# A hybrid decoder layer on one core: the low parts of the up projection's weights, subtracted by VectorE or added by a transfer

## The chip, the cores and the metric

The kernel runs on one core of a Trainium2 chip. The metric is the time of one execution on the device in microseconds. A core has a matrix engine (TensorE, PE in the profile), a vector engine (VectorE, DVE), a scalar engine (ScalarE, ACT), a general engine (GpSimd, POOL) and a synchronization engine (SyncE, SP). Each works through its own list of instructions in order, and semaphores make one wait for another. SP and GpSimd also start transfers (DMAs) between the outer memory and the memory on the chip; 16 DMA engines carry them out.

## The reference, cut to what matters

One step of a decoder layer for 512 prompt rows and 8 sample rows, 520 in all. After three mixing branches and a first layer norm comes a gated feed-forward block:

```
h = layer_norm(ALPHA * x + merged @ w_o)                     # 520 x 1024
u = causal_dwconv(h @ w_ffn_in, width 3)                     # 520 x 5632
f = (silu(u[..., :D_FF]) * u[..., D_FF:]) @ w_ffn_out        # D_FF = 2816
out = layer_norm(ALPHA * h + f)
```

All of it is in float32. The change concerns the weights of `h @ w_ffn_in`, the gated product's up projection.

## The kernel before

Everything stands transposed: features on the 128 partitions, the 520 rows along the free dimension, in two halves of 260 columns.

TensorE multiplies in a rounded float32 format (fp32r). To keep the precision, every operand is split into a rounded high part and a low part that holds the rest, and every product is three matmuls: high by high, high weight by low data, low weight by high data (`mm3`, where line 357 issues the matmul). `split` makes the parts: ScalarE rounds the source into `hi` by a copy (`act`, line 161), VectorE subtracts it from the source into `lo` (`tt`, line 164).

The up projection has 5632 output features, that is 44 units of 128. A unit's weights are a tile of 128 x 1024: eight blocks of 128 x 128. Per unit, `wunit` loads the tile by a transfer on SP's queue into `raw` (line 241; two buffers), and `wsplit` splits it into `whi` and `wlo` (two buffers each). Then come 48 matmuls: 2 halves by 8 blocks by 3. A unit can be split when TensorE is through with the unit two before, whose buffers it takes. When `raw` has been read for the last time, SP loads the unit after next, and behind it starts a copy of a piece of a cache (line 219) that has nothing to do with the unit.

The result of each half is evicted by ScalarE twice (`ffn_evac`): a plain copy `fu` and a scaled one `fy`. `ffn_taps` adds the two other taps of the width-3 convolution on VectorE (line 167) and has GpSimd copy ten columns aside (line 1465). Units come in pairs, gate and up; `silu` on ScalarE and a product on VectorE follow, and the result is split into `f` for the down projection.

The first six units (`NH`, the list `early`) are special. They are loaded and split while the first layer norm still runs, two into `whi` and `wlo`, four into spare tiles named `wz`, each as two halves of 128 x 512. Their matmuls are done for the first 260 columns and then for the second, so that TensorE has work while the second half is normalized. The layer norm (`proj_ln`) writes its rows into `r`, rounds them on ScalarE into `h_hi` and subtracts on VectorE into `h_lo`.

The order on each engine is set when the program is built: a scheduler with a model of times places the instructions by priority (`hp` gives weight splits and evictions a high one, the dense matmuls have a low one).

Of the kernel before, what the change touches and what calls it, by code (L numbers as in the profile page):

```python
# [12 lines left out]
ALU = mybir.AluOpType  # L13
# [103 lines left out]
def build(tc, nc, I, O):  # L117
    V, S, T, G = nc.vector, nc.scalar, nc.tensor, nc.gpsimd
# [11 lines left out]
    def hp(more=0):  # L130
        return tc.high_priority(HP + more)
# [13 lines left out]
    def z2(name, shape=(128, NT), dt=F32):  # L145
        return pool.tile(list(shape), dt, tag="z", bufs=NZ, name=name)
# [13 lines left out]
    def act(out, in_, func=AF.Copy, **kw):  # L160
        return S.activation(out, in_, func, **kw)  # L161

    def tt(out, a, b, op):
        return V.tensor_tensor(out, a, b, op=op)  # L164
# [50 lines left out]
    def cache_step(n=1):  # L215
        for _ in range(n):
            pc = next(pieces, None)
            if pc is not None:
                nc.sync.dma_start(*pc)

    nload, last_split, quiet = [0], [None], [False]

    def split(hi, lo, src):
        act(hi, src)
        return tt(lo, src, hi.bitcast(F32), ALU.subtract)
# [12 lines left out]
    def wload(src, n):  # L238
        raw = wp.tile([128, 8, 128], F32, tag="raw", bufs=2, name="raw")
        with tc.issue_after(x_load.ins):  # L240
            ins = nc.sync.dma_start(raw[:, :n].rearrange("p k m -> p (k m)"), src)
        nload[0] += 1
        if nload[0] > 1 and late:
            with tc.issue_after(ins.ins):
                late.popleft()()
        elif nload[0] > 6:
            with tc.issue_after(ins.ins):
                cache_step(0 if quiet[0] else 3 if nload[0] % 4 == 0 else 1)
        return raw

    def wsplit(raw, n, where=None):

        if where is None:
            where = [[wp.tile([128, 8, 128], F32R, tag=t, name=t) for t in ("whi", "wlo")]]
        ks, k0 = [], 0
        for hi, lo in where:
            m = min(hi.shape[1], n - k0)
            if m > 0:
                last_split[0] = split(hi[:, :m], lo[:, :m], raw[:, k0:k0 + m])
                ks += [(hi[:, k], lo[:, k]) for k in range(m)]  # L260
            k0 += m
        return ks

    def wunit(src, n, where=None):
        with hp():
            return wsplit(wload(src, n), n, where)

    def wz(*allocs):

        return [[alloc("wz", (128, 4, 128), F32R) for _ in range(2)] for alloc in allocs]  # L270
# [18 lines left out]
    def P(name, i=0, n=1):  # L289
        o = PPO[name] + i  # L290
        return pp[:, o:o + n]
# [68 lines left out]
    def dps(n=2):  # L360
        return [pd.tile([128, 512], F32, tag="d", name="ps")[:, :HB] for h in range(n)]


    def densemm(ps, w, X, first=True, last=True, halves=(0, 1)):
        with tc.high_priority(-LOW):
            mm3(ps, w, X, first, last, halves)

    def dense(w, X):
        ps = dps()
        densemm(ps, w, X)  # L370
        return ps
# [3 lines left out]
    def zchunk():  # L375
        i = zi[0]
        zi[0] += 1
        w = w0 if i == 0 else wunit(I['wz'][i], 8)
        return dense(w, XS)
# [744 lines left out]
    def stream_dense():  # L1124
# [61 lines left out]
        def branch(i, js, na):  # L1186
            br = B_ORDER[i]
            wn, X, n, ev = outs[br]
            ahead = []
            for j in js[:na]:  # L1190
                ahead.append(gate(br, j))
                yield 6.5
            yield ('w', ev)
            for j in js:
                gt = ahead[j] if j < len(ahead) else gate(br, j)
                w = wunit(I[wn][j], n)
                pb = dense(w, X)
                if i == 0:
                    mg.append(gt)
                if i == 2:  # L1200
                    XM.append((t2(f"m{j}h", dt=F32R), t2(f"m{j}l", dt=F32R)))
                with hp():
                    for h in range(2):
                        stt(gt[:, HS[h]], gt[:, HS[h]], 1.0, pb[h], ALU.add, ALU.mult)

                for sl in HS if i == 2 and j == 7 else (slice(0, NT),):
                    if i:
                        tt(mg[j][:, sl], mg[j][:, sl], gt[:, sl], ALU.add)
                    if i == 2:
                        hi, lo = [x[:, sl] for x in XM[j]]  # L1210
                        act(hi, mg[j][:, sl], scale=0.5)
                        last_m[0] = stt(lo, mg[j][:, sl], 0.5, hi.bitcast(F32), ALU.mult, ALU.subtract)
                yield 6.5 + 0.8 * n
# [214 lines left out]
    XH = [(h_hi[:, j, :], h_lo[:, j, :]) for j in range(8)]  # L1428
# [4 lines left out]
    def wo_unit(j):  # L1433
        q = j - nF1
        where = wz(z2, z2) if 2 <= q < 6 else wz(t2, t2) if q == 6 else wz(a2, a2) if q == 7 else None

        quiet[0] = True
        with ExitStack() as es:
            if j:
                es.enter_context(tc.issue_after(last_m[0].ins))  # L1440
            r = [(wunit(I['wo'][j], 8, where), 0)]
        quiet[0] = False
        if j in range(1, 6):
            nc.sync.dma_start(rr[j + 1], I['xT'][:, j + 1, :])
        return r
# [18 lines left out]
    def ffn_taps(c, u, y):  # L1464
        G.tensor_copy(nu[:, c, :], u[:, 510:520])  # L1465
        tt(y[:, 512:520], y[:, 512:520], sfs[:, c, :], ALU.add)
        stt(y[:, 1:512], u[:, 0:511], P('fdw', c * 3 + 1), y[:, 1:512])
        stt(y[:, 2:512], u[:, 0:510], P('fdw', c * 3 + 0), y[:, 2:512])

    def ffn_evac(c, u, y, ps, halves):  # L1470
        with hp():
            for h, p_ in zip(halves, ps):
                act(u[:, HS[h]], p_)
            for h, p_ in zip(halves, ps):
                act(y[:, HS[h]], p_, AF.Identity, scale=P('fdw', c * 3 + 2), bias=P('fdb', c))

    early = []
    for i in range(NH):
        early.append((wunit(I['wfi'][i], 8, (wz(t2, a2) if i > 3 else wz(z2, z2)) if i >= 2 else None), z2("fu"), z2("fy")))
    for h in range(2):  # L1480
        for i in range(NH):
            w, u, y = early[i]
# [7 lines left out]
    def ffn_chunk(c, i):  # L1490
        if i < NH:
            _, u, y = early[i]
        else:
            u, y = z2("fu"), z2("fy")
            ffn_evac(c, u, y, dense(wunit(I['wfi'][i], 8), XH), (0, 1))
        ffn_taps(c, u, y)
        return y

    for i in range(22):
        yg = ffn_chunk(i, 2 * i)  # L1500
        act(yg, yg, AF.Silu)
        yu = ffn_chunk(22 + i, 2 * i + 1)
        tt(yg, yg, yu, ALU.mult)
        hi, lo = [t(f"f{i}", dt=F32R) for t in FT[i]]
        split(hi, lo, yg)
        XF.append((hi, lo))
# [123 lines left out]
```

## Time and profile before

| | |
|---|---|
| time, median of 3 runs | 1019.94 us (1019.75 to 1020.02) |
| profiled execution | 1019.17 us, its span 1017.4 us |
| TensorE busy | 991.1 us (97%) |
| VectorE busy | 712.7 us (70%) |
| ScalarE busy | 498.1 us (49%) |
| GpSimd busy | 217.6 us (21%) |
| mean granted clock of TensorE | 0.992 |
| moved by DMA | 153.07 MB, mean 150 GB/s |

The span is the time from the first to the last instruction of the profiled execution. Busy times are sums over the span, so an engine with a low share can still be the one that is waited for in some stretch. Matmuls overlap: one is shown with 0.28 us while the next starts 0.12 us later. The granted clock is given as a share of the full 2.4 GHz.

### The profile page before, as it was taken

The numbers are of one execution on the slowest core, as the hardware profiler recorded it, in microseconds if no ns is written. First come the engines' busy times: TensorE is split into PE (matmuls) and PEld (weight loads), VectorE is DVE, ScalarE is ACT, GpSimd is POOL, SyncE is SP. The second block draws the span as 40 slices with busy tenths as digits, with TensorE's granted clock in tenths as the row PEclk, the third lists the DMA queues.
The fourth block names the chain that finished last, engine by engine and source line by source line (L and its number), as shares of the span: only waits on it lengthen the run. The fifth ranks groups of instructions, "written<-read, shape, count | busy, mean of one in ns | idle before, by whom it ended". The sixth has DMA issues, their size and how long they took to land.

```text
span 1017.4 us, 22069 instructions
## 1 busy us (share of the span) xinstructions
PE 991.1 (97%) x8979; PEld 965.6 (95%) x8979; DVE 712.7 (70%) x1335; ACT 498.1 (49%) x1029; POOL 217.6 (21%) x313
## 2 busy tenths in 40 slices
PE   7999999999999999999999998999999999999994
PEld 7999999999999899989999997999999999999994
DVE  5999899996587589873657888655565655423286
ACT  6345843574453444355543466555555555312154
POOL 0131355363414533321011000111111111000000
PEclk9999999999999999999999998999999999999998
DMA  7543356666536767564346441134334343332322
GB/s 245 198 158 119 135 170 216 208 193 230 190 102 180 242 213 247 158 194 140 120 138 241 151 166 63 53 115 139 116 123 143 115 140 114 113 95 81 96 74 84
DMA packets 48501, 153.07 MB, mean 150 GB/s; under 512 B 9808, under 2 KB 13456, under 8 KB 45328
## 3 DMA queue, kind: packets, MB, share of 16 engines
q1 hardware_dynamic: 35520, 113.15, 33.9%
q0 software_dynamic: 12880, 38.52, 11.7%
q8 instruction: 70, 1.15, 0.5%
q14 instruction: 31, 0.25, 0.1%
HBM read 132.02 MB, written 46.81 MB: 176 GB/s over the span
## 4 chain that ended last, share of the span: by engine, by line
PE 82%; DVE 7%; DMA 4%; issue 3%; ACT 3%; POOL 1%; SPq 0%; ACTq 0%; POOLq 0%; DVEq 0%
PE ps L357 72%; DVE r L167 1%; DVE wlo L164 1%; PE lor L423 1%; PE at L640 1%; ACT whi L161 1%; DVE vx L164 1%; DMA raw<-in_wrw_dram 1%; DMA swk<-in_swkv_dram 0%; PE q L794 0%; PE pt L496 0%; PE st L821 0%; DMA sct<-nd 0%; DMA raw<-in_wz_dram 0%; PE btp L655 0%
## 5 line engine op out<-in xcount | busy, mean ns | idle before, releaser
L357 PE MATMUL ps<-x_hi,whi 128*128 128x260 f32 x1024 | 292.2, 285 | 5.6 <-ACT whi L161 5.5
L357 PE MATMUL ps<-x_lo,whi 128*128 128x260 f32 x1024 | 293.0, 286 | 0.3 <-DVE x_lo L164 0.2
L357 PE MATMUL ps<-x_hi,wlo 128*128 128x260 f32 x1024 | 292.5, 286 | 0.4 <-DVE wlo L164 0.4
L164 DVE TENSOR_TENSOR wlo<-raw,whi 128x1024 fp32r<-128x1024 f32 (+2 forms) x152 | 168.4, 1108 | 173.2 <-ACT whi L161 172.4
L161 ACT ACTIVATE whi<-raw 128x1024 fp32r<-128x1024 f32 (+2 forms) x152 | 146.9, 967 | 221.6 <-PE ps L357 195.7
L357 PEld LDWEIGHTS ps<-x_hi,whi 128*128 128x128 f32 x1024 | 193.6, 189 | 6.9 <-ACT whi L161 5.5
L357 PEld LDWEIGHTS ps<-x_hi,wlo 128*128 128x128 f32 x1024 | 194.0, 189 | 2.4 <-DVE wlo L164 1.0
L357 PEld LDWEIGHTS ps<-x_lo,whi 128*128 128x128 f32 x1024 | 193.4, 189 | 1.8 <-DVE x_lo L164 1.1
L357 PE MATMUL ps<-h_lo,whi 128*128 128x260 f32 x640 | 182.1, 284 | 4.0 <-DVE h_lo L164 4.0
L357 PE MATMUL ps<-h_hi,whi 128*128 128x260 f32 x640 | 181.2, 283 | 0.0
L357 PE MATMUL ps<-h_hi,wlo 128*128 128x260 f32 x640 | 180.6, 282 | 0.0
L357 PEld LDWEIGHTS ps<-h_lo,whi 128*128 128x128 f32 x640 | 120.7, 189 | 4.6 <-DVE h_lo L164 4.4
L357 PEld LDWEIGHTS ps<-h_hi,wlo 128*128 128x128 f32 x640 | 121.1, 189 | 0.1
L357 PEld LDWEIGHTS ps<-h_hi,whi 128*128 128x128 f32 x640 | 120.6, 188 | 0.0
L357 PE MATMUL ps<-f,whi 128*128 128x260 f32 x592 | 107.2, 282 | 0.0
L1465 POOL COPY nu<-fu 128x10 f32<-128x10 f32 x44 | 40.3, 916 | 270.9 <-ACT fu L161 270.9
L357 PEld LDWEIGHTS ps<-f,whi 128*128 128x128 f32 x592 | 91.4, 188 | 0.1
L167 DVE SCALAR_TENSOR_TENSOR acc<-u,pp,acc 128x511 f32<-128x511 f32 (+29 forms) x120 | 84.3, 733 | 0.4
L357 PE MATMUL ps<-f,wlo 128*128 128x260 f32 x296 | 83.6, 283 | 0.0
L167 DVE SCALAR_TENSOR_TENSOR fy<-fu,pp,fy 128x511 f32<-128x511 f32 x88 | 65.8, 747 | 1.5
L357 PEld LDWEIGHTS ps<-f,wlo 128*128 128x128 f32 x296 | 55.7, 188 | 0.0
L161 ACT ACTIVATE fu<-ps 128x260 f32<-128x260 f32 x88 | 33.0, 377 | 43.4 <-PE ps L357 43.3
(549 smaller groups left out, 1841.3 us busy)
## 6 DMA issues: line engine op xcount, KB each, us to landing
raw<-in_wz_dram SPq DMA_DIRECT2D x63, 512.0 KB, 3.7
raw<-in_wfi_dram SPq DMA_DIRECT2D x44, 512.0 KB, 3.5
out_dram<-in_cc_dram SPq DMA_DIRECT2D x128, 128.0 KB, 3.5
rl<-d POOLq DMA_DIRECT2D x32, 256.0 KB, 4.9
raw<-in_wfo_dram SPq DMA_DIRECT2D x16, 512.0 KB, 3.6
out_dram<-in_cb_dram SPq DMA_DIRECT2D x56, 146.0 KB, 3.7
d<-at POOLq DMA_DIRECT2D x16, 256.0 KB, 3.6
raw<-in_wo_dram SPq DMA_DIRECT2D x8, 512.0 KB, 3.7
```

The source lines that it names most:

```text
L161: return S.activation(out, in_, func, **kw)
L164: return V.tensor_tensor(out, a, b, op=op)
L167: return V.scalar_tensor_tensor(out, a, s, b, op0=op0, op1=op1)
L357: last_mm[0] = T.matmul(ps[i], lhsT=a, rhs=x[:, HS[h]], start=first and k == 0 and q == 0, stop=last and k == len(w) - 1 and q == 2)
L423: T.matmul(ps, lhsT=lor[l][w][:, p, :], rhs=X[x][:, HS[h]], start=i == 0, stop=i == len(wx) - 1)
L640: T.matmul(pst[par][:, c * 128:(c + 1) * 128], lhsT=bk[o:o + 64, c].rearrange("p a b -> p (a b)"), rhs=kr[o:o + 64, c].rearrange("p a b -> ...
L1465: G.tensor_copy(nu[:, c, :], u[:, 510:520])
```

## The change

For the 44 units of the up projection the low part is made in another way. Before, VectorE computed `lo = raw - hi`. Now ScalarE, after rounding `raw` into `hi`, makes a second pass and writes the negative of the same rounded value into `lo`; then GpSimd starts a transfer that reads the unit's weights from the outer memory once more and adds them onto `lo`, so that it holds `raw - hi` when the transfer has landed. The splits of all other weights and of the data are as before. The outer memory is read for 44 x 512 KB more.

```diff
-    def wsplit(raw, n, where=None):
+    def wsplit(raw, n, where=None, src=None):
...
             if m > 0:
-                last_split[0] = split(hi[:, :m], lo[:, :m], raw[:, k0:k0 + m])
+                w = raw[:, k0:k0 + m]
+                if src is None:
+                    last_split[0] = split(hi[:, :m], lo[:, :m], w)
+                else:
+                    act(hi[:, :m], w)
+                    act(lo[:, :m], w, scale=-1.0)
+                    G.dma_start(lo[:, :m].rearrange("p k m -> p (k m)"), src[:, k0 * 128:(k0 + m) * 128],
+                                accum_op=ALU.add)
...
-    def wunit(src, n, where=None):
+    def wunit(src, n, where=None, add=False):
         with hp():
-            return wsplit(wload(src, n), n, where)
+            return wsplit(wload(src, n), n, where, src if add else None)
...
     for i in range(NH):
-        early.append((wunit(I['wfi'][i], 8, (wz(t2, a2) if i > 3 else wz(z2, z2)) if i >= 2 else None), z2("fu"), z2("fy")))
+        early.append((wunit(I['wfi'][i], 8, (wz(t2, a2) if i > 3 else wz(z2, z2)) if i >= 2 else None,
+                            0 <= i <= 5), z2("fu"), z2("fy")))
...
-            ffn_evac(c, u, y, dense(wunit(I['wfi'][i], 8), XH), (0, 1))
+            ffn_evac(c, u, y, dense(wunit(I['wfi'][i], 8, add=6 <= i <= 43), XH), (0, 1))
```

First place: ScalarE in the middle of the up projection, two units. Before, it held this, with `whi` the rounding of a unit, `fu` and `fy` the evictions of one half, and `f` and the second `fy` parts of the gating:

```order
L161 ACTIVATE f_9528<-fy 128x520 [waits DVE_49]
L161 ACTIVATE whi<-raw 128x1024 [waits DMAHW2_49,PE_49]
L161 ACTIVATE fu<-ps 128x260 [waits PE_49]
L161 ACTIVATE fy<-ps,pp 128x260
L161 ACTIVATE fu<-ps 128x260 [waits PE_49,Pool_49]
L161 ACTIVATE fy<-ps,pp 128x260
L161 ACTIVATE fy<-fy 128x520 [waits DVE_49,Activation_49]
L161 ACTIVATE whi<-raw 128x1024 [waits DMAHW4_49,PE_49]
```

Now it holds this, at the same place of the stage:

```order
L161 ACTIVATE whi<-raw 128x1024 [waits DMAHW4_49,PE_49]
L161 ACTIVATE fu<-ps 128x260 [waits PE_49]
L161 ACTIVATE fy<-ps,pp 128x260
L161 ACTIVATE wlo<-raw 128x1024 [waits DMASW1_49,Activation_49]
L161 ACTIVATE fu<-ps 128x260 [waits PE_49,Pool_49]
L161 ACTIVATE fy<-ps,pp 128x260
L161 ACTIVATE fy<-fy 128x520 [waits DVE_49,Activation_49]
L161 ACTIVATE whi<-raw 128x1024 [waits DMAHW6_49,PE_49]
```

The pass into `wlo` stands behind one pair of evictions, three instructions after the rounding.

Second place: GpSimd in the same stage, where before there stood 44 copies into `nu` and nothing between them. Now transfers (`DMA wlo<-in_wfi_dram`) alternate with the copies:

```order
L1473 COPY nu<-fu 128x10 [waits Activation_49]
L266 DMA wlo<-in_wfi_dram 128x1024 [waits DMASW1_49,PE_49,Activation_49]
L1473 COPY nu<-fu 128x10 [waits Activation_49]
L266 DMA wlo<-in_wfi_dram 128x1024 [waits DMASW2_49,PE_49,Activation_49]
L1473 COPY nu<-fu 128x10 [waits Activation_49]
```

Each transfer waits for ScalarE's pass. On TensorE the order in this stage is the one of before, but the first matmul of a unit that reads `wlo` now waits for a transfer (DMASW) where it waited for VectorE.

Third place: VectorE in the first layer norm, from the variance of the first half (`lrs<-lv,lm`) on. Before:

```order
L167 SCALAR_TENSOR_TENSOR lrs<-lv_7893,lm_8211 128x260 [waits PE_49]
L167 SCALAR_TENSOR_TENSOR r_7809<-ld_7892,r_7809 128x260
L164 TENSOR_TENSOR lsq<-lsq 128x260 [waits Activation_49]
L167 SCALAR_TENSOR_TENSOR r_7809<-r_7809,ps 128x260 [waits PE_49]
L164 TENSOR_TENSOR wlo<-raw,whi 128x1024 [waits DMAHW4_49,Activation_49]
L164 TENSOR_TENSOR r_7809<-r_7809,cn 128x260 [waits DVE_49]
L1373 RECIPROCAL lrs<-lrs 128x260 [waits Activation_49]
L164 TENSOR_TENSOR wz<-raw,wz 128x512 [waits DMAHW6_49,Activation_49]
```

Now:

```order
L167 SCALAR_TENSOR_TENSOR lrs<-lv_7893,lm_8211 128x260 [waits PE_49,Activation_49]
L167 SCALAR_TENSOR_TENSOR r_7805<-ld_7892,r_7805 128x260
L167 SCALAR_TENSOR_TENSOR r_7807<-ld_7892,r_7807 128x260
L167 SCALAR_TENSOR_TENSOR r_7809<-ld_7892,r_7809 128x260
L164 TENSOR_TENSOR lsq<-lsq 128x260 [waits Activation_49]
L167 SCALAR_TENSOR_TENSOR r_7809<-r_7809,ps 128x260 [waits PE_49]
L1381 RECIPROCAL lrs<-lrs 128x260 [waits Activation_49]
L164 TENSOR_TENSOR r_7809<-r_7809,cn 128x260 [waits DVE_49]
```

The subtractions into `wlo` and `wz` are gone from between the norm's own steps, and the variance comes ahead of two steps that it followed.

## Rows read from the trace of the kernel before

**Rows 1.** The page's head and its first part, busy us of each engine.

```profile
span 1017.4 us, 22069 instructions
PE 991.1 (97%) x8979; PEld 965.6 (95%) x8979; DVE 712.7 (70%) x1335; ACT 498.1 (49%) x1029; POOL 217.6 (21%) x313
```

**Rows 2.** Windows: stretch, length, busy of each engine, PEclk, DMA share, GB/s.

```profile
600.00:606.00 6.00, 6.00 (x52) 6.00 (x51) 5.99 (x12) 4.10 (x10) 0.00 (x0) 1.00 0.68 224
606.00:612.00 6.00, 6.00 (x52) 6.00 (x51) 6.00 (x16) 4.36 (x12) 0.00 (x0) 1.00 0.42 147
...
655.00:862.00 207.00, 207.00 (x1729) 207.00 (x1729) 123.27 (x182) 117.38 (x216) 34.19 (x36) 1.00 0.37 123
```

**Rows 3.** ScalarE's timeline at one unit: start us, duration us, what [idle before].

```profile
701.30 1.06 ACT L161 ACTIVATE whi<-raw 128x1024 fp32r<-128x1024 f32 x1 [1.18 <-PE ps L357]
702.26 0.37 ACT L161 ACTIVATE fu<-ps 128x260 f32<-128x260 f32 x1
702.53 0.56 ACT L161 ACTIVATE fy<-ps,pp 128x260 f32<-128x260 f32 x1
...
707.05 1.06 ACT L161 ACTIVATE whi<-raw 128x1024 fp32r<-128x1024 f32 x1 [0.50 <-PE ps L357]
```

**Rows 4.** VectorE's timeline at the same unit.

```profile
702.39 1.23 DVE L164 TENSOR_TENSOR wlo<-raw,whi 128x1024 fp32r<-128x1024 f32 x1 [3.00 <-ACT whi L161]
```

**Rows 5.** TensorE's timeline, two matmuls in a row of an up projection unit.

```profile
623.40 0.28 PE L357 MATMUL ps<-h_hi,wlo 128*128 128x260 f32 x1
623.52 0.28 PE L357 MATMUL ps<-h_hi,whi 128*128 128x260 f32 x1
```

**Rows 6.** Tile wlo in 655 to 860: duration ns min/median/max, first and last start.

```profile
L357 PE MATMUL ps<-h_hi,wlo x569: 277/282/286, 655.4 to 859.7; 128*128 128x260 f32 x190
L164 DVE TENSOR_TENSOR wlo<-raw,whi x35: 1224/1226/1229, 662.1 to 857.7; 128x1024 fp32r<-128x1024 f32 x35
```

**Rows 7.** ScalarE's timeline: the rounding of unit 6.

```profile
640.89 1.06 ACT L161 ACTIVATE whi<-raw 128x1024 fp32r<-128x1024 f32 x1 [4.79 <-PE ps L357]
```

**Rows 8.** VectorE's timeline in the layer norm: one whole and one half subtraction.

```profile
598.18 1.22 DVE L164 TENSOR_TENSOR wlo<-raw,whi 128x1024 fp32r<-128x1024 f32 x1 [0.49 <-ACT whi L161]
...
602.92 0.69 DVE L164 TENSOR_TENSOR wz<-raw,wz 128x512 fp32r<-128x512 f32 x1
```

**Rows 9.** TensorE's waits: whom for, us in total, times, longest.

```profile
PE ps L357 <- DVE h_lo L164: 4.0, 2, 3.3
```

**Rows 10.** TensorE's timeline at these waits.

```profile
613.48 0.39 PE L357 MATMUL ps<-h_lo,whi 128*128 128x260 f32 x1 [0.72 <-DVE h_lo L164]
613.71 0.28 PE L357 MATMUL ps<-h_hi,wlo 128*128 128x260 f32 x1
613.82 0.36 PE L357 MATMUL ps<-h_hi,whi 128*128 128x260 f32 x1
617.45 0.59 PE L357 MATMUL ps<-h_lo,whi 128*128 128x260 f32 x1 [3.26 <-DVE h_lo L164]
```

**Rows 11.** Windows after these waits.

```profile
616.00:620.00 4.00, 2.16 (x6) 1.67 (x7) 4.00 (x12) 2.56 (x7) 0.00 (x0) 0.50 0.72 229
620.00:624.00 4.00, 4.00 (x20) 3.51 (x19) 2.19 (x6) 1.67 (x5) 0.00 (x0) 0.67 0.01 4
```

**Rows 12.** GpSimd's timeline at the unit of rows 3.

```profile
702.69 0.98 POOL L1465 COPY nu<-fu 128x10 f32<-128x10 f32 x1 [4.78 <-ACT fu L161]
```

**Rows 13.** DMA issues: queue, count, size of each, median us from issue to landing.

```profile
raw<-in_wfi_dram SPq DMA_DIRECT2D x44, 512.0 KB, 3.5
...
raw<-in_wfo_dram SPq DMA_DIRECT2D x16, 512.0 KB, 3.6
...
raw<-in_wcv_dram SPq DMA_DIRECT2D x8, 256.0 KB, 2.8
...
nd<-scr POOLq DMA_DIRECT2D x1, 512.0 KB, 4.1
...
sct<-nd POOLq DMA_DIRECT2D x1, 256.0 KB, 8.7
```

**Rows 14.** SP's timeline at the unit of rows 3.

```profile
703.64 0.33 SPq L241 DMA_DIRECT2D raw<-in_wfi_dram  x1
```

## The prediction, made before the changed kernel ran

> **What bounds the kernel now.** I read the page's first part, then the busy times by stretch, then the timelines of one unit of the stage that changes. TensorE is busy in 991.1 of 1017.4 us [rows 1], and in the stage of the up projection, 655 to 862 us, in all of 207.00 us, while VectorE has 123.27 and ScalarE 117.38 [rows 2]. So a microsecond taken off VectorE there is worth nothing by itself; a microsecond put in front of TensorE costs a microsecond. The other place that matters is the layer norm before it: at 600 to 612 us VectorE is busy in 5.99 and 6.00 of each 6 us [rows 2], and shortly after TensorE waits for it.
>
> One unit (a weight tile of 128x1024, 48 matmuls) takes 5.75 us: the rounding of unit i starts at 701.30 and that of unit i+1 at 707.05, each when TensorE is through with the buffer of the unit two before [rows 3]. Two buffers of each kind take turns, so unit i-1 runs on TensorE from about 701.3 to 707.05, and within this time unit i must be made ready. Before, VectorE subtracts at 702.39 for 1.23 us [rows 4]: ready at 703.62. Every unit's matmuls come as high, high, low, spaced 0.12 us [rows 5], so the low part is read first at 707.05 + 0.24 = 707.29. The slack is 3.7 us, and no unit of the stage waits for its weights.
>
> **The change part by part.**
>
> *Removed:* 44 subtractions on VectorE. 36 of them (units 8 to 43; 35 show in the window, 1.226 us each [rows 6]) lie in the stage where TensorE never waits for VectorE: worth 0. The other eight units come earlier. Unit 6 is rounded at 640.89 [rows 7] and its low part first read at 655.4 [rows 6], and unit 7 is much the same: 0. Units 0 to 5 are split inside the crowded layer norm: two of 1.22 us and eight halves of 0.69 us [rows 8], 8.0 us of VectorE where TensorE waits 4.0 us for the low part of the normalized rows [rows 9], the longer of these waits ending at 617.45 [rows 10]. The granted clock is 0.50 in 616 to 620 and 0.67 in 620 to 624 [rows 11]; 0.67 over 4 us means half clock until about 622.6, so 5.2 us after 617.45 ran at half speed, 1.2 instead of 2.4 GHz: 2.6 us lost. At best 4.0 + 2.6 = 6.6 us come back. Against that ScalarE gets as many extra passes there (two of 1.06, eight of about 0.6: 6.9 us), in front of its own rounding of those rows; at worst all 6.9 us delay TensorE. I take half of the best, 3 us of gain.
>
> *Added on ScalarE:* one more pass of 1.06 us a unit [rows 3]. In the stage that makes 117.4 + 36 x 1.06 = 156 of 207 us, so it does not bind by itself. But it stands in the path of the low part, and behind the two evictions of the unit two before, as the order shows.
>
> *Added on GpSimd's queue:* a transfer of 512 KB a unit that adds onto the low tile. It can only be issued when the second pass is done, and TensorE's third matmul now waits for its landing. Its own queue does not hold it up: the copy between two transfers is done at 702.69 + 0.98 = 703.67 [rows 12], before the pass it stands ahead of is over.
>
> The path: rounding 701.30, evictions 702.26 and 702.53, the second taking 0.56 to 703.09 [rows 3], second pass 1.06 to 704.15, 0.06 from ScalarE to GpSimd (702.63 to 702.69 [rows 3, 12]): issue at 704.21. With another 0.06 for the wait at the end, the landing may take 707.29 - 704.21 - 0.06 = 3.0 us and no more. Call D what it takes.
>
> If D is over 3.0, unit i starts D - 3.0 late. Unit i+1 is not late a second time: its buffer came free at the end of unit i-1, before this gap, so its low part arrives with the same delay and finds unit i still running. So the pattern is two units back to back, then a gap: **18 gaps of D - 3.0 us for 36 units.**
>
> *D.* The trace has no adding transfer. The nearest rows [rows 13]: a plain 512 KB load on SP's queue lands in 3.5 us; a plain 512 KB one on GpSimd's in 4.1 (there is one); the slowest listed on it 8.7. Moving time is seen by size: 256 KB in 2.8 and 512 KB in 3.6 us on the same queue, so 1.6 us for 512 KB. An addition must fetch the old bytes besides the new: 1.6 more. And the next raw load, 512 KB, is issued by the same event (raw is read for the last time by what makes the low part: 703.64, against the subtraction's end at 703.62 [rows 14, 4]), so the two share the engines: between 0 and 1.6, I take 0.8. D = 4.1 + 1.6 + 0.8 = 6.5 us. Lower end 4.1, upper end 8.7 + 1.6 = 10.3.
>
> The Trainium skill puts the movement lower: "DMA: Bandwidth & Descriptors", section "Anatomy of one DMA — SWDGE (gpsimd) path", fits 2.0 us plus bytes over 436 GB/s, 3.2 us for 512 KB as an estimate; the one row here says 4.1 and decides. "Collectives: The Full Stack", section "The bandwidth ceiling: the fold count and why AG ≠ RS ≠ AR", says that the sum itself is free but its two reads halve the rate; no run here shows that yet. By both, D would be 2.0 + 2 x 1.2 = 4.4 us, 18 x 1.4 = 25 us of gaps and 1041 us by estimate, which is inside rival A below.
>
> *The clock.* A pause of 3.26 us with a handful of matmuls and 0.72 us before it brought the clock down and cost 2.6 us [rows 10, 11]. Gaps of 3.5 us between full stretches are of that size, but shorter than the whole pause there. I take a third of the 18: 6 x 2.6 = 16 us; the ends are 0 and 18 x 2.6 = 47.
>
> **Sum:** 18 x (6.5 - 3.0) = 63, plus 16, minus 3: +76 us. The profiled execution took 1019.17 us (1.8 around its span), the median is 1019.94, so 1095 by the one and **1096 us** by the other.
>
> **Rivals.**
>
> *A. The transfer is light.* D between 3.5 and 5.2: the old bytes come out of on-chip memory beside the new ones, at no price, and the raw load is no hindrance. 18 x 0.5 to 18 x 2.2, no falls of the clock, 0 to 7 back: about 1019 to 1060. For it: the plain row of 4.1. Against: it must move more bytes than that row and beside another load.
>
> *B. The transfer is heavy.* D over 8 (an add that goes by smaller pieces, or many bytes waiting in turn): every gap over 5 us, and the clock falls in each. From 18 x 5.0 + 47 - 3 = +134 to 18 x 7.3 + 47 + 7 = +185: 1153 to 1204. For it: GpSimd's transfers of 256 KB have taken up to 8.7. Against: that one is the slowest of the list.
>
> *C. Faster.* D at 3.0 or below: the stage costs nothing, and what is left is the relief of VectorE in the layer norm, up to 6.6 us: 1013 to 1019. It decides from D = 3.0. For it: VectorE is full there and TensorE waits. Against: even the plain load on SP's queue takes 3.5.
>
> *D. ScalarE binds.* 4.3 us of work in a unit of 5.75: no, unless its queue order makes a rounding wait behind a slow eviction; it would add at most the second pass, 1.06 x 36 = 38 us, and only where the transfer is hidden. I count it into A's and the forecast's upper ends.
>
> **How the numbers follow.** The forecast, D from 5.2 to 8, has its own range of 18 x 2.2 - 3 = +37 to 18 x 5.0 + 47 - 3 = +134, 1057 to 1153, with 0.58. A 0.16, B 0.20, C and a tie 0.06 (C itself 0.04). To hold eight in ten I go down through most of A and half of B: 1036 to 1185. Within 0.2% (2 us, about what a measurement of this kernel can tell from no change) I give 0.02, faster 0.04, slower 0.94.
>
> **What would show it.** In the profile after: TensorE busy in clearly less than all of the stage, with gaps whose releaser is the transfer into the low tile, in every second unit, third matmul; the chain of waits with a share for that transfer; the transfer's median landing, which is D; the granted clock below 1.00 in the stage or not, which settles the clock's term; VectorE some 50 us lighter, ScalarE some 45 heavier; TensorE's wait for the low rows at 613 to 617 shorter than 4.0. I am wrong if the landing is at 3 us or under, or if gaps come with every unit and not with every second one (then the price doubles), or if the early units' transfers land late for the first half and add a wait there.

## The result and the profile after

The changed kernel takes 1148.55 us (median of 3 runs, 1147.74 to 1148.74) against 1019.94: a ratio of 1.1259 [1.1234, 1.1285], 12.6% slower. The prediction said 1096 us; its range of 1036 to 1185 holds the time, and so does the forecast's own range of 1057 to 1153.

First the page of the changed kernel: its head, the busy times, the clock by slices, the chain that ended last by engine and by line, and two groups of instructions (busy us and mean ns, then the idle time before them and its releaser). They answer to [rows 1].

```profile
span 1146.9 us, 22199 instructions
...
PE 1031.0 (90%) x8979; PEld 1001.9 (87%) x8979; DVE 662.0 (58%) x1287; ACT 535.7 (47%) x1077; POOL 230.3 (20%) x361
...
PEclk9999999999999999999999988988888888999998
...
PE 68%; DMA 15%; DVE 6%; ACT 6%; issue 4%; POOL 0%; SPq 0%; ACTq 0%; DVEq 0%; POOLq 0%
PE ps L365 60%; DMA wlo<-in_wfi_dram 12%; ACT wlo L161 1%; DMA raw<-in_wfi_dram 1%; DVE wlo L164 1%; ACT whi L161 1%; PE lor L431 1%; PE at L648 1%; DVE r L167 1%; ACT fy L161 1%; DVE vx L164 1%; DMA raw<-in_wrw_dram 1%; ACT fu L161 1%; PE pt L504 0%; PE st L829 0%
...
L365 PE MATMUL ps<-h_hi,wlo 128*128 128x260 f32 x640 | 199.6, 312 | 89.9 <-DMA wlo<-in_wfi_dram 85.2
...
L1473 POOL COPY nu<-fu 128x10 f32<-128x10 f32 x44 | 11.3, 257 | 283.7 <-ACT fu L161 283.3
```

The span grew by 129.5 us. VectorE lost 50.7 us of work and ScalarE gained 37.6 (some 50 and some 45 were forecast), and neither is what the kernel waits for: the new entry is a transfer, 12% of the chain, and TensorE stands idle for 89.9 us in front of the matmuls that read `wlo`. How often, in TensorE's waits (us in total, times, longest):

```profile
PE ps L365 <- DMA wlo<-in_wfi_dram: 85.2, 17, 5.6
...
PE ps L365 <- ACT f L161: 4.7, 1, 4.7
...
PE ps L365 <- DVE h_lo L164: 1.2, 1, 1.2
```

17 waits carry the transfer's name. The one on `f` stands in front of the same kind of matmul at the same place of a unit, and it too ends 0.13 us after a transfer has landed, as the 17 do, so it belongs to them: 18 pauses, 89.9 us, 5.0 each, in 36 units. The last line answers to [rows 9], where it was 4.0. One pause in the chain of waits (start us, us, what):

```profile
754.16 0.14 ACT whi L161
754.30 0.82 issue
755.12 0.37 ACT fu L161
755.49 0.46 ACT fy L161
755.95 0.96 ACT wlo L161
756.91 0.29 issue
757.20 7.64 DMA wlo<-in_wfi_dram
764.83 0.14 issue
764.97 7.18 PE ps L365 x45
```

This is the path of the prediction, with the steps of [rows 3] and the pass behind the evictions: rounding, two evictions, second pass, transfer, third matmul. From the rounding at 754.16 to the issue at 757.20 are 3.04 us, where 2.91 were forecast. The pause at the end of this piece:

```profile
764.97 0.36 PE L365 MATMUL ps<-h_hi,wlo 128*128 128x260 f32 x1 [4.75 <-DMA wlo<-in_wfi_dram]
```

The transfer took 7.64 us here and the pause is 4.75, so 2.9 us were covered. What is longer than forecast is the transfer's landing, in the list of DMA issues (KB each, median us from issue to landing), which answers to [rows 13]:

```profile
raw<-in_wfi_dram SPq DMA_DIRECT2D x44, 512.0 KB, 4.8
wlo<-in_wfi_dram POOLq DMA_DIRECT2D x40, 512.0 KB, 8.1
```

8.1 us instead of 6.5, and 8.1 - 3.0 = 5.1 is a pause of 5.0 as nearly as a median can tell. The raw load beside it went from 3.5 to 4.8. The clock, around the pause that ended at 746.00 (columns as in [rows 2]: behind the stretch's length come the busy times of the five engines, then the granted clock):

```profile
740.00:746.00 6.00, 0.74 (x8) 0.56 (x6) 2.28 (x4) 2.74 (x4) 1.07 (x2) 0.89 0.88 193
746.00:748.00 2.00, 2.00 (x9) 2.00 (x10) 0.00 (x0) 0.00 (x0) 0.00 (x0) 0.50 0.47 156
...
750.00:752.00 2.00, 2.00 (x13) 2.00 (x12) 0.00 (x0) 0.86 (x3) 0.00 (x0) 0.61 0.62 127
752.00:754.00 2.00, 2.00 (x19) 2.00 (x18) 0.70 (x1) 0.51 (x1) 0.00 (x0) 1.00 0.02 2
...
660.00:990.00 330.00, 240.09 (x1689) 236.86 (x1688) 81.39 (x143) 146.95 (x249) 38.45 (x72) 0.87 0.58 133
```

After the pause TensorE is busy in all of each 2 us but starts only half as many matmuls: it runs at 1.2 GHz until about 751.6. Over the whole stage the clock is 0.87, where [rows 2] has 1.00. What that costs comes from two pairs of rows on ScalarE, the roundings of units 8 and 43, which stand at the two ends of the same work; before:

```profile
661.02 1.06 ACT L161 ACTIVATE whi<-raw 128x1024 fp32r<-128x1024 f32 x1 [0.93 <-PE ps L357]
...
862.39 1.06 ACT L161 ACTIVATE whi<-raw 128x1024 fp32r<-128x1024 f32 x1 [1.18 <-PE ps L357]
```

and after:

```profile
660.35 1.06 ACT L161 ACTIVATE whi<-raw 128x1024 fp32r<-128x1024 f32 x1 [0.85 <-PE ps L365]
...
985.54 1.06 ACT L161 ACTIVATE whi<-raw 128x1024 fp32r<-128x1024 f32 x1 [1.31 <-PE ps L365]
```

325.2 us against 201.4: 123.8 more. 17 of the 18 pauses lie in it, and 89.9 less the last one's 3.8 is 86.1; the other 37.7 us, 2.2 for each pause, are put down to the clock. The granted clock itself says the same: it fell behind each of the 18 pauses, by turns for longer and for shorter, as in these two stretches of 7 us:

```profile
783.30:790.30 7.00, 7.00 (x37) 7.00 (x38) 0.48 (x1) 1.37 (x3) 0.00 (x0) 0.59 0.65 155
802.20:809.20 7.00, 6.97 (x45) 7.00 (x46) 0.70 (x1) 1.37 (x3) 0.00 (x0) 0.76 0.65 144
```

A clock of 0.59 over 7 us loses 2.9 us, one of 0.76 loses 1.7; over all 18 such stretches it is 39 us. Behind unit 43's rounding the kernel is 6.3 us longer than before: the last pause of 3.8, and 2.5 with its fall of the clock. Ahead of unit 8's it is 0.7 us earlier. These three stretches make up the whole of the 129.5, and pauses and clock explain nearly all of it.

### The profile page after: what moved, and what is told of

The parts are those of the page before. It is cut to its first block, busy times and chain, and to the rows that moved or that the text cites. A ratio compares the mean times of both kernels' runs of the same rounds, so it can differ in the third digit from the quotient of the medians.

```text
span 1146.9 us, 22199 instructions
## 1 busy us (share of the span) xinstructions
PE 1031.0 (90%) x8979; PEld 1001.9 (87%) x8979; DVE 662.0 (58%) x1287; ACT 535.7 (47%) x1077; POOL 230.3 (20%) x361
## 3 DMA queue, kind: packets, MB, share of 16 engines
q1 hardware_dynamic: 35520, 113.15, 31.5%
## 4 chain that ended last, share of the span: by engine, by line
PE 68%; DMA 15%; DVE 6%; ACT 6%; issue 4%; POOL 0%; SPq 0%; ACTq 0%; DVEq 0%; POOLq 0%
PE ps L365 60%; DMA wlo<-in_wfi_dram 12%; ACT wlo L161 1%; DMA raw<-in_wfi_dram 1%; DVE wlo L164 1%; ACT whi L161 1%; PE lor L431 1%; PE at L648 1%; DVE r L167 1%; ACT fy L161 1%; DVE vx L164 1%; DMA raw<-in_wrw_dram 1%; ACT fu L161 1%; PE pt L504 0%; PE st L829 0%
## 5 line engine op out<-in xcount | busy, mean ns | idle before, releaser
L365 PE MATMUL ps<-h_hi,wlo 128*128 128x260 f32 x640 | 199.6, 312 | 89.9 <-DMA wlo<-in_wfi_dram 85.2
L365 PEld LDWEIGHTS ps<-h_hi,wlo 128*128 128x128 f32 x640 | 138.3, 216 | 93.1 <-issue 83.0
L365 PE MATMUL ps<-h_hi,whi 128*128 128x260 f32 x640 | 197.8, 309 | 0.1
L365 PE MATMUL ps<-h_lo,whi 128*128 128x260 f32 x640 | 196.7, 307 | 1.2 <-DVE h_lo L164 1.2
L164 DVE TENSOR_TENSOR wlo<-raw,whi 128x1024 fp32r<-128x1024 f32 (+3 forms) x112 | 119.1, 1063 | 97.1 <-ACT whi L161 96.6
L365 PEld LDWEIGHTS ps<-h_hi,whi 128*128 128x128 f32 x640 | 138.3, 216 | 1.1 <-ACT h_hi L161 1.0
L365 PEld LDWEIGHTS ps<-h_lo,whi 128*128 128x128 f32 x640 | 137.7, 215 | 1.6 <-DVE h_lo L164 1.5
L164 DVE TENSOR_TENSOR fy<-fy,sfs 128x8 f32<-128x8 f32 x44 | 7.3, 167 | 141.6 <-ACT fy L161 141.6
L164 DVE TENSOR_TENSOR f<-fy,f 128x520 fp32r<-128x520 f32 x22 | 15.4, 700 | 120.1 <-ACT f L161 120.1
L1473 POOL COPY nu<-fu 128x10 f32<-128x10 f32 x44 | 11.3, 257 | 283.7 <-ACT fu L161 283.3
```

Of the source, the lines that this page charges most:

```text
L365: last_mm[0] = T.matmul(ps[i], lhsT=a, rhs=x[:, HS[h]], start=first and k == 0 and q == 0, stop=last and k == len(w) - 1 and q == 2)
```

## The experiments

The theory: the loss is the lateness of an adding transfer, D - 3.0 us in every second unit with D = 8.1, plus a fall of the clock after each pause. What had to be tested was the pattern (why every second unit), what makes D 8.1 (the addition, the raw load at the same moment, the copies of the caches on SP's queue, ScalarE's pass), and the clock. Every edit below is made on the changed kernel; ratios are to the kernel before, run on the same chip in the same series.

**Only the early units.** Units 0 to 5 add, the others subtract as before.

```diff
-            ffn_evac(c, u, y, dense(wunit(I['wfi'][i], 8, add=6 <= i <= 43), XH), (0, 1))
+            ffn_evac(c, u, y, dense(wunit(I['wfi'][i], 8, add=False), XH), (0, 1))
```

> Only the six early units (0 to 5) get their low parts by the adding transfer; units 6 to 43 have VectorE's subtraction again. Theory (the price is the landing in the steady stage, the layer norm's relief is a small gain): no gaps in the up projection, TensorE waits for the low rows of the norm 1.2 us instead of 4.0 as in the full change, 1016 to 1019 us. Rival (the early units' transfers and passes cost as well, hidden so far by the rest): 1021 us or more.

1018.66 us, ratio 0.9985 [0.9973, 0.9998], an interval that only just ends below 1. All of the loss lies in units 6 to 43, and the half of the change inside the layer norm is a small gain of about 1.5 us. TensorE's waits in its profiled execution, with 1022.52 us one of the longest of the twelve:

```profile
PE ps L365 <- DVE h_lo L164: 1.9, 2, 1.2
```

4.0 us became 1.9 [rows 9], where 1.2 were expected: VectorE's relief shortens the wait. Of the versions tried, this is the only one that is not slower than the kernel before.

**Every second unit.** Units 8, 10, 12, ... add, the others subtract.

```diff
-            ... dense(wunit(I['wfi'][i], 8, add=6 <= i <= 43), XH) ...
+            ... dense(wunit(I['wfi'][i], 8, add=i < 8 or i % 2 == 0), XH) ...
```

> Adding transfers for units 0 to 7 and for the even units from 8 on; the odd units from 9 on have VectorE's subtraction. 18 of 36 transfers of the stage are gone, but every one left follows the unit two before in the same buffer. Theory (a gap per pair of units, since the transfer has only one unit's time beside it): the 18 gaps stay, 1138 to 1150 us. Rival (each transfer has its own price, 129 us over 36): half of it, about 1084 us.

**Two of four units.** As many transfers, on neighbouring units.

```diff
-            ... dense(wunit(I['wfi'][i], 8, add=6 <= i <= 43), XH) ...
+            ... dense(wunit(I['wfi'][i], 8, add=i < 8 or i % 4 < 2), XH) ...
```

> As many adding transfers as in the run with every second unit (18 in the stage), but in pairs: units 8, 9, 12, 13, 16, 17 and so on add, the others subtract on VectorE. Theory: the second of each pair is hidden behind the first one's gap, so 9 gaps of about 5 us with 2 us of clock each: 1078 to 1086 us. If time went by the number of transfers, this run and the one with every second unit would agree.

The two were run together. With every second unit: 1148.99 us, 1.1263 [1.1243, 1.1282]. With pairs: 1087.70 us, 1.0662 [1.0643, 1.068]. TensorE's waits, of the first and of the second:

```profile
PE ps L365 <- DMA wlo<-in_wfi_dram: 89.7, 18, 5.6
```

```profile
PE ps L365 <- DMA wlo<-in_wfi_dram: 48.4, 9, 6.2
```

Leaving out half of the transfers changed nothing, and moving the other half next to each other brought back 61 us with the same number of transfers. So the price hangs on pauses, not on transfers: where two neighbours are late together, the second is free. A load spread over all units (ScalarE's passes, bytes moved) would have been halved in both. The pairs came out 2 us over the expectation: their pauses are 48.4 / 9 = 5.4 us long, not 5.0, since their landing is slower (8.5 us in the median of all).

**A plain transfer.** The transfer overwrites the low part instead of adding to it; all else stays.

```diff
-    G.dma_start(lo[...], src[:, k0 * 128:(k0 + m) * 128], accum_op=ALU.add)
+    G.dma_start(lo[...], src[:, k0 * 128:(k0 + m) * 128])
```

> The changed kernel with a plain transfer instead of an adding one: the low part is overwritten by the weights, so the addition is left out; order, sizes and queue are the same. My own sum puts the landing at 4.1 + 0.8 = 4.9 us: gaps of 1.9 us, hardly a fall of the clock, 1050 to 1060 us. Rival (not the addition but the company of the raw load and the cache copies makes 8.0 us): landing 7 us or more, 1120 us or more.

1069.92 us, 1.0488 [1.0469, 1.0506].

```profile
wlo<-in_wfi_dram POOLq DMA_DIRECT2D x40, 512.0 KB, 5.2
```

The addition accounts for 2.9 us of the landing (8.1 to 5.2) and about 79 us of the time; the plain transfer's own lateness makes the other 50. The time missed the expectation by 10 us: the landing was 5.2 and not 4.9, which is 5 us over 18 pauses, and the clock, of which hardly a fall was expected, cost some 10 us.

TensorE's waits put 31.5 us down to the transfer, in 22 pauses, and 9.4 to ScalarE, 6.2 of them to evictions, which looks like rival D. It isn't. One of them, the transfer that its matmul needs and the eviction that it is put down to:

```profile
762.79 0.53 POOL L266 DMA_DIRECT2D wlo<-in_wfi_dram  x1 [1.45 <-ACT wlo L161]
769.31 0.56 ACT L161 ACTIVATE fy<-ps,pp 128x260 f32<-128x260 f32 x1
769.98 0.36 PE L364 MATMUL ps<-h_hi,wlo 128*128 128x260 f32 x1 [1.58 <-ACT fy L161]
```

This transfer took 7.05 us and landed at 769.84, and TensorE went on 0.14 us later, as behind the other landings; the eviction happened to end in between, at 769.87. So it is with every pause over 0.3 us in this stage, in this run and in the next: each ends 0.13 or 0.14 us after a landing. Here there are 26, together 40.6 us: the sum's 18 x (5.2 - 3.0) = 40 has their total but not their number. Why the lateness spreads over neighbouring units here is not shown.

**The addition alone.** Units 8 to 43 use the raw tile of unit 7, so that neither the raw loads nor the copies of the caches run beside the adding transfers.

```diff
-            ... dense(wunit(I['wfi'][i], 8, add=6 <= i <= 43), XH) ...
+            ... dense(wunit_held(i), XH) ...
...
```

> The changed kernel in which units 8 to 43 split the raw tile of unit 7 over and over: their 36 raw loads and the cache copies behind them are left out, so the adding transfer has no company. If company costs it what it cost the plain one (5.2 against 4.1 us), it lands in 6.9 us: gaps of 3.6 us, 65 us instead of 90, and fewer falls of the clock, 1095 to 1122 us. Rival (the addition itself is all of it): 8.0 us and 1145 us or more.

**Without the cache copies.** The raw loads stay; the copies that `wload` drains beside them are left out from unit 8 on.

```diff
-            ... dense(wunit(I['wfi'][i], 8, add=6 <= i <= 43), XH) ...
+            quiet[0] = i >= 8
+            w = wunit(I['wfi'][i], 8, add=6 <= i <= 43)
+            quiet[0] = False
+            ... dense(w, XH) ...
```

> The changed kernel with the cache copies behind the raw loads of units 8 to 43 left out, the raw loads kept. If it is the raw load that stands in the way: landing 7.6 us or more, 1138 us or more; if the copies: 7.2 us or less, 1130 us or less.

Alone: 1087.66 us, 1.0646 [1.0559, 1.0733]. Without the copies: 1147.59 us, 1.1233 [1.1162, 1.1303]. The landings, first alone, then without the copies:

```profile
wlo<-in_wfi_dram POOLq DMA_DIRECT2D x40, 512.0 KB, 5.6
```

```profile
wlo<-in_wfi_dram POOLq DMA_DIRECT2D x40, 512.0 KB, 7.8
```

The theory expected 6.9 alone and 1095 us or more, and was wrong; so was the rival's 8.0. Without the copies the time came out as expected for the raw load. The raw load of 512 KB, issued within 0.3 us of the adding transfer, costs it 2.2 us (5.6 to 7.8); the copies of 128 KB behind it only 0.3 (7.8 to 8.1).

**A third pair of buffers.** Units 8, 11, ... 29 are split into a spare pair of tiles that is free until then, so that a unit's split can start one unit earlier.

```diff
-            ... wunit(I['wfi'][i], 8, add=6 <= i <= 43) ...
+            ... wunit(I['wfi'][i], 8, wz(a2, a2) if i in range(8, 30, 3) else None, 6 <= i <= 43) ...
```

> The changed kernel with a third pair of weight buffers for units 8 to 30 (every third unit takes four spare tiles, in two halves), so that an adding transfer has two units' time beside it, 8.8 us. Theory: no gaps up to unit 30, then 6 or 7 of the 18, 1066 to 1076 us, though the transfers land as late as before. Rival (the transfers come as fast as the queue can carry them): no change, 1145 us or more.

1067.05 us, 1.0444 [1.0379, 1.051]. TensorE's waits and the landings:

```profile
PE ps L365 <- DMA wlo<-in_wfi_dram: 32.7, 13, 5.3
```

```profile
wlo<-in_wfi_dram POOLq DMA_DIRECT2D x32, 512.0 KB, 8.2
wz<-in_wfi_dram POOLq DMA_DIRECT2D x24, 256.0 KB, 9.4
```

The transfers land no sooner, yet only 45 of the 129 us are left. From 660 to 760 us, where every third unit has the spare pair, TensorE waits 2.5 us in all; behind unit 30 the pauses return, six of 3.7 to 5.3 us, as expected. So what falls short with two buffers is the time beside the transfer, 3.0 us; with three it is one whole unit more.

**The pauses filled.** 36 spare matmuls, whose result nobody reads, stand in front of the first low matmul of units 8, 10, 12, ...

```diff
+                    if fill[0] and q == 1:
...
+                        for _ in range(fill[0]):
...
+                                last_mm[0] = T.matmul(spare[:, :HB], lhsT=hi, rhs=xh[:, HS[0]], start=True, stop=True)
...
+            fill[0] = 36 if i >= 8 and i % 2 == 0 else 0
```

> The changed kernel with 36 idle matmuls (4.3 us, into a spare tile that nobody reads) before the first low matmul of every even unit from 8 on, where the gaps of 5 us are. If the loss beyond the gaps is the clock falling after a pause, the granted clock stays at 1.00 in the stage and the time falls by the 38 us that it cost: 1106 to 1114 us. Rival (the slow matmuls behind a gap have another cause, such as the transfers' traffic): no gain, 1145 us or more.

1116.39 us, 1.0927 [1.0866, 1.0988]. The stage in one window:

```profile
660.00:960.00 300.00, 287.81 (x2356) 284.65 (x2356) 82.60 (x145) 149.76 (x252) 38.32 (x72) 0.99 0.65 149
```

TensorE does 36 x 18 = 648 matmuls more for nothing and the kernel is 32 us faster than the changed one. The pauses are still there as time, but the clock stays at 0.99. The pauses' total did not change: 18 x 4.3 us of spare matmuls and 10.9 us of waits behind them are 88 us, where it was 89.9. So the 32 us (34, each kernel against its own runs of the kernel before) are the clock's share measured by itself, most of the 38 to 40 us read from the traces. The time came out 2 us over the expectation, and the clock is not wholly at 1.00.

**The negative pass first.** ScalarE writes the negative low part before it rounds the high part, so the transfer is issued a pass earlier, and ahead of the raw load.

```diff
-act(hi[:, :m], w)
-act(lo[:, :m], w, scale=-1.0)
+neg = act(lo[:, :m], w, scale=-1.0)
 G.dma_start(lo[...], ..., accum_op=ALU.add)
+with tc.issue_after(neg.ins):
+    act(hi[:, :m], w)
```

> The changed kernel with ScalarE's two passes swapped: it writes the negative low part first, behind the same two evictions, and rounds the high part after it. The adding transfer is issued one pass (1.0 us) earlier, and the next raw load, which waits for the last reading of the raw tile, no longer at the same moment but about 0.7 us after it. Theory (the gap is the landing less what lies beside it; company costs by overlap): the landing at 7.0 to 8.0 us, cover 4.0 instead of 3.0, gaps of 3.0 to 4.0 us with fewer falls of the clock, 1085 to 1125 us. Rival (another wait comes last as soon as the transfer is earlier, or the load takes its turn as before): 1140 us or more.

1104.06 us, 1.0817 [1.0774, 1.086]. A piece of its chain of waits, its stage, and the landings of the raw load and of the transfer:

```profile
711.94 0.96 ACT wlo L161
712.90 0.29 issue
713.19 6.88 DMA wlo<-in_wfi_dram
```

```profile
660.00:946.00 286.00, 229.14 (x1706) 224.93 (x1705) 80.80 (x143) 145.68 (x251) 37.46 (x71) 0.92 0.63 152
```

```profile
raw<-in_wfi_dram SPq DMA_DIRECT2D x44, 512.0 KB, 6.7
wlo<-in_wfi_dram POOLq DMA_DIRECT2D x40, 512.0 KB, 7.2
```

The raw load is now issued 0.7 us after the transfer (713.87), which lands in a median of 7.2 us instead of 8.1, while the load takes 6.7 instead of 4.8: which of the two goes first decides in part which one pays. Of TensorE's 58.6 us of waits, 58.2 are 18 pauses of 3.2 us. That is 1.8 less than in the changed kernel: 0.9 by the landing, and the rest about the one pass by which the transfer is issued earlier. Together they give back a third of the loss; no run changes the one without the other.

The clock did not fall behind all of these pauses, but behind 13 of the 18. Two stretches of 7 us, one without a fall and one with:

```profile
688.60:695.60 7.00, 7.00 (x58) 7.00 (x59) 0.98 (x3) 2.71 (x6) 0.19 (x1) 1.00 0.72 171
703.80:710.80 7.00, 7.00 (x46) 7.00 (x47) 0.70 (x1) 1.37 (x3) 0.00 (x0) 0.76 0.80 206
```

## Why the prediction was right, and which terms were off

*The direction and the path* hold: TensorE is the bound, VectorE's subtractions were worth nothing in the stage, and the transfer into the low tile took the place of the subtraction as what ends last.

*The pattern*, 18 pauses of D - 3.0 us, holds to 0.1 us a pause: there are 18, in every second unit at its third matmul, 5.0 us each with D = 8.1. The cover of 3.0 us, worked out from [rows 3, 5, 12], is 2.9 in the trace. The two experiments with half of the transfers confirm that a neighbour is free. With the short pauses of the plain transfer and of the addition alone the total still holds, while the pauses are 26 and 23.

*D* was the term that was off most. "Between 0 and 1.6, I take 0.8" for the company of the raw load: measured 2.2, and 2.5 with the cache copies, above the upper end given for this term. The other part, 4.1 + 1.6 = 5.7 for an addition alone, measured 5.6; how near is in part luck, for the one plain row of 4.1 took 3.5 to 3.8 us in nine of the eleven traces. The 1.6 was the time that the raw load's own bytes take to move, as if it delayed its neighbour by no more than that. The plain transfer lost between 1.1 and 1.7 in the same company (to 5.2, from 4.1 or 3.5), the adding one 2.2, and with the adding one issued first, the load pays more and it pays less. Why the adding one pays more than the load's moving time stays open: that it is longer in motion and so meets its neighbour for longer is a guess that no run tested. D makes the pauses 89.9 us instead of 63, 27 of the 53 us by which the forecast missed.

The Trainium skill's rule that the sum is free and its two reads halve the rate ("Collectives: The Full Stack", section "The bandwidth ceiling: the fold count and why AG ≠ RS ≠ AR"), which the page states of a collective's reduction, agrees with the run alone: 5.6 - 4.1 = 1.5 us more for the addition (2.1 with 3.5 for the plain row), beside 1.6 us of moving time for 512 KB. The 1041 us worked out from the pages' figures did not come: alone the transfer took 5.6 us and not 4.4, and the figures count no neighbour and no fall of the clock.

*The clock*: the price of a fall was nearly right (2.6 taken, 2.2 measured), the number was not. "I take a third of the 18": it fell after each of the 18, 40 us instead of 16. Only a part of this follows from D. Rival B had said that it would fall in each with D over 8; but with the negative pass first, at pauses of 3.2 us, shorter than the 3.5 of the forecast, it fell after 13 of 18, and the loss beyond the pauses is 84.0 - 58.6 = 25 us. So a third was too few for the forecast's own pauses, too. The granted clock behind each pause, run by run: it fell after all 18 pauses of 5.0 us, 13 of 18 of 3.2, 7 of 23 of 2.2 (alone) and 5 of 26 of 1.6 (plain transfer). What grows with the pause is how often it falls; a fall costs about 2 us in each of these runs, by the loss beyond the pauses.

*The layer norm*: 3 us of gain were taken. The wait for `h_lo` went from 4.0 to 1.2, unit 8's rounding came 0.7 us earlier, although the first weight load of the up projection is issued 1.5 us later than before (586.50 against 584.98), and the early units alone gain 1.5 us. Right in sign, and 1.5 to 2.3 us smaller. The early transfers did not land late: TensorE has no wait for one.

*ScalarE*: not a bound, as said; 37.6 us more against about 45. Rival D did not occur even where the pauses are short.

The sum, then: 63 + 16 - 3 became 90 + 40 - 1. The mechanism was right, but both large terms were too small, so the wide range held the time and the sum did not. By its conditions, D over 8 and a fall of the clock in each pause, the case is at the lower edge of rival B; that the time is 4 us under B's 1153 and inside the forecast's own range is luck, for it comes from the price of a fall, 2.2 us instead of 2.6.

## What to carry to other kernels

Price a transfer that enters a tight stage together with what is issued by the same event: measure it beside its neighbour, and don't take the neighbour's own moving time as the upper end (here 2.2 us were paid, and the neighbour's bytes move in 1.6). Look at which of the two is issued first. Count pauses rather than transfers: with two buffers, two units late together cost one pause, and half of the transfers cost as much as all of them or half as much, according to which half. A third buffer gave back 84 of 129 us though no transfer landed sooner. A pause on TensorE can have a second price, paid at half clock after it; here it was paid more often the longer the pauses were, so add it. Where a wait is put down to an engine, see whether a transfer landed at the same moment.

## What the runs showed of the hardware that was not expected

- An adding transfer is dearer to issue too. GpSimd is busy for 0.88 us with it, and 0.53 with a plain one of the same 512 KB; the row of a plain one stands with its run (762.79), this is the changed kernel's:

```profile
757.20 0.88 POOL L266 DMA_DIRECT2D wlo<-in_wfi_dram  x1 [1.45 <-ACT wlo L161]
```

- From ScalarE's end to GpSimd's issue passes 0.29 us, and not the 0.06 taken from a copy that waited for ScalarE.
- GpSimd's copies of 128 x 10 take 257 ns in the mean in the changed kernel (the group `nu<-fu` above), 0.19 us each in the stage, where [rows 12] had 0.98. VectorE's subtraction, which ran at that moment, is what makes the difference. The run with every second unit has both kinds: the copy takes 0.97 us beside a subtraction, and ends with it, and 0.19 in a unit without one.

```profile
704.24 1.23 DVE L164 TENSOR_TENSOR wlo<-raw,whi 128x1024 fp32r<-128x1024 f32 x1 [3.33 <-ACT whi L161]
704.54 0.97 POOL L1473 COPY nu<-fu 128x10 f32<-128x10 f32 x1 [3.22 <-ACT fu L161]
717.13 0.19 POOL L1473 COPY nu<-fu 128x10 f32<-128x10 f32 x1 [11.62 <-ACT fu L161]
```

- Spare matmuls on a waiting TensorE made the changed kernel 32 us faster, by the clock: 0.99 in the stage instead of 0.87.
